# The opening of a hybrid attention and PEER layer: where the adaLN sums, the low parts and the loads are placed

## The chip, the cores and the metric

The kernel runs on one core of a Trainium2 chip. The metric is the device time of one execution in microseconds (us), the median of several runs.

## The reference, cut to what matters

One decoder layer for 256 tokens of width 1024, in float32. The part that the change touches is the opening:

```python
mod = silu(c) @ w_ada + b_ada                # (6144): sh1, sc1, g1, sh2, sc2, g2
h = rms_norm(x, norm_attn) * (1 + sc1) + sh1
proj = h @ w_in                              # MoBA q|k|v, DSA q|k|v, indexer q|k|weights
y = concat(moba_attention(...), dsa_attention(...)) @ w_out    # 16 heads of 64
x = x + g1 * y
h = rms_norm(x, norm_ffn) * (1 + sc2) + sh2
x = x + g2 * peer_ffn(h, ...)                # scores, top 16 of 256 per head, 16384 experts
out = rms_norm(x, norm_final)
```

With 256 tokens MoBA is plain causal attention; DSA keeps for each token the 64 keys that the indexer scores highest.

## The kernel before

Tokens stand along the free dimension: x is `xT`, eight tiles (c = 0 to 7) of 128 features by 256 tokens. Products that need float32 precision are done as three matmuls of rounded operands (`mm3`, lines 127 to 130): each operand is split into a high part, a rounded copy made by ScalarE (line 109), and a low part, the remainder, made by VectorE or GpSimd (line 111). `lo_engine` (line 100) names the engine of the low part of weight tile k: GpSimd for k below 9 and for 12 to 16, VectorE for the rest up to the PEER weights.

All weights come through one stream, `seq`, of 128 x 1024 tiles (512 KB), in four buffers `raw`; `load_next` issues the next one, `ahead` and `take` issue loads and splits some tiles ahead of their use. All these loads and those of `w_ada` are issued by SyncE, in order. A load that waits for its buffer holds all behind it. The first tiles of `seq` are two pairs of q and k (k = 0 to 3, the "early" tiles), four tiles of V's left half (4 to 7), and then, in the order of `ORDER`, the indexer's three and the pairs of the later heads.

`silu(c) @ w_ada` is a sum over eight chunks (128 rows of w_ada by 1024 columns, one of six parts). `ada_step` (lines 216 to 220) adds one chunk, scaled per partition by `sc`, to an accumulator on VectorE; a column of ones on TensorE then sums over the partitions (`ada_end`, line 327, which leaves mod in columns), and line 330 adds the bias. For the scale part (part 1) chunks 0 and 2 go to TensorE as rows instead (`ada_rows`, line 314) and are turned into columns at line 321.

The opening is written in a fixed order per engine (`tc.manual_schedule()`). It computes the squares' sum and the root `rstd`; the scale part, full chunks; then, half by half (four of the eight c), `xa_half`: VectorE makes xa = x * amul * rstd (line 365), ScalarE its high part xh (line 366), VectorE or for two of the c GpSimd its low part xl (line 363). `early_mm` multiplies the four early tiles with xa, before the shift is known; the shift's share is added later through `early_shift` (line 347, the shift as two columns) and `early_cols` (line 354), as a bias per output row. The shift part (part 0) is summed in column halves of 512, all eight chunks on VectorE; after each half `sh_half` makes the shifted h as hi (line 256) and lo (line 257). V's first tiles are multiplied between these (`vproj_steps`). The early products of tile 3 stand behind the first half's column sum in TensorE's order; V's second tile stands behind the second's.

`early_cols` ends the room of the early tiles; the attention's `bias` tile takes that room, and its two loads (1 MB each, from a small table `frd` in DRAM, which holds the bias by distance) follow there.

Behind the opening the framework's planner orders the instructions of each engine from the program's order and a model of their times. The program's order is `ORDER`: A computes q and k of a pair of heads, S the softmax, B the values, I, N and T the indexer's projections, norm and top-k (64 of 256 by eight rounds of max and replace), V the right half of V, D2, D3 and D4 the VectorE sums of the other modulation parts (part 2 is g1, 3 and 4 belong to the second norm), E their transposes and reduces (`ada_half`, lines 235 to 238). Then come the output projection, the second norm, PEER's scores and routing, and two long loops over 128 tiles of U and of V (lines 912, 913 and 128 to 130).

Of the kernel before, what the change touches and what calls it, by code (L numbers as in the profile page):

```python
# [16 lines left out]
T = 256  # L17
# [27 lines left out]
def hybrid_kernel(ctx, tc, io, out):  # L45
# [14 lines left out]
    def bank_a():  # L60
        return bank("pa", 2)
# [44 lines left out]

# [49 lines left out]

    def first_load(part, half, c):
        a, n = (0, 1024) if part else (half * 512, 512)
        w = first_w[part, half, c] = w0.tile([128, n], FT, tag=f"wada{part}", name="wada", bufs=6 if part else 10)
        col = part * 1024 + a  # L160
        nc.sync.dma_start(w, io["w_ada"][c * 128:(c + 1) * 128, col:col + n])

    for c in range(8):
        first_load(1, 0, c)
        if c in W_AT[0]:
            load_next()
    for half in range(2):
        for c in range(8):
            if c in W_AT[1 + half]:
                load_next()  # L170
            first_load(0, half, c)
# [126 lines left out]
    def ada_dve(part, half, chunks, w=None):  # L298

        for c in chunks:  # L300
            x = first_w[part, half, c]
            o = acc1 if part else acc0[:, half * 512:half * 512 + 512]
            if w is not None:
                x, o = x[:, w], o[:, w]
            ada_step(o, x, c, c == next(i for i in range(8) if i not in ADA_PE[part, half]))

    def ada_rows(part, half, cols):

        p = bank("c3" if half else "c2")
        chunks = ADA_PE[part, half]  # L310
        row = pf.tile([1, 512], FT, tag="row", name="row", bufs=2)
        for c in chunks:
            w = first_w[part, 0 if part else half, c]
            nc.tensor.matmul(p[0:1, :], sc[:, c:c + 1], w[:, half * 512:half * 512 + 512] if part else w,
                             start=(c == chunks[0]), stop=(c == chunks[-1]))
            yield None
        nc.scalar.activation(row, p[0:1, :], AF.Copy)
        yield None
        for q in range(4):
            w = slice(q * 128, q * 128 + 128)  # L320
            nc.tensor.matmul(cols[:, q:q + 1], row[:, w], ones[0:1, 0:1], start=(q == 0), stop=False, skip_group_check=True)
        yield None

    def ada_end(part, half, cols):

        for q in range(4):
            nc.tensor.matmul(cols[:, q:q + 1], (acc1 if part else acc0)[:, (half * 4 + q) * 128:(half * 4 + q + 1) * 128],
                             ones[:, 0:1], start=(q == 0 and not ADA_PE[part, half]), stop=(q == 3), skip_group_check=True)
        s = slice(part * 8 + half * 4, part * 8 + half * 4 + 4)
        nc.vector.tensor_tensor(mod[:, s], cols[:, 0:4], bada[:, s], op=OP.add)  # L330

# [24 lines left out]

    def xa_half(half):
        s = slice(half * 4, half * 4 + 4)
        m = slice(8 + half * 4, 12 + half * 4)
        nc.vector.scalar_tensor_tensor(amul[:, 0, s], mod[:, m], 1.0, nat[:, s], op0=OP.add, op1=OP.mult)  # L360

        def low(c):
            (nc.vector if XL_DVE[c] else nc.gpsimd).tensor_tensor(xl[:, c, :], xa[:, c, :], xh[:, c, :].bitcast(FT), op=OP.subtract)
        for c in range(half * 4, half * 4 + 4):
            nc.vector.scalar_tensor_tensor(xa[:, c, :], xT[:, c, :], amul[:, 0, c:c + 1], rstd, op0=OP.mult, op1=OP.mult)
            nc.scalar.activation(xh[:, c, :], xa[:, c, :], AF.Copy)
            if c % 4:
                low(c - 1)
        low(c)
# [20 lines left out]
    next(r10); next(r11)  # L390
    busy(BUSY1)
    next(r10); next(r11)
    busy(BUSY1)
    fps = bank_a()
    nc.tensor.matmul(fps[:16, :256], rbT, oh, start=True, stop=True)
    ada_dve(1, 0, (3,))
    rstd = next(rs)
    ada_dve(1, 0, (4, 5, 6))
    next(r10); next(r11)
# [12 lines left out]
    ada_end(1, 1, pc[1][:, 4:8])
    xa_half(1)
    early_ps = [bank_b(), bank_b(), bank("c0"), bank("c1")]
    early_mm(0, 0)
    early_mm(1, 0)
    early_mm(0, 1)
    early_mm(1, 1)
    early_split()
    early_mm(2, 0)  # L420
    early_mm(2, 1)
    early_split()
    ada_dve(0, 0, range(8))
    cols0 = bank("c2")
    ada_end(0, 0, cols0)
    ada_dve(0, 1, range(0, 2))
    early_mm(3, 0)
    early_mm(3, 1)
    sh_half(0)
    ahead(6, 2)  # L430
    shp = bank("c3")
    early_shift(0)
    ada_dve(0, 1, range(2, 8))
    cols1 = bank("c2")
# [630 lines left out]
```

## Time and profile before

| | us |
|---|---|
| median of 3 runs | 1030.16 (1029.49 to 1030.53) |
| the profiled execution | 1031.32 |
| its span, first to last instruction | 1029.50 |

```profile
PE 988.0 (96%) x5695; PEld 842.5 (82%) x5695; DVE 786.4 (76%) x1588; ACT 634.5 (62%) x1411; POOL 58.4 (6%) x78
PE   8888999989899999999999999999999999999996
DVE  5948987689999988888888898767555555555556
POOL 2442210000300000000000000000000000000000
PEclk8789989999999999999999999999999999999998
```

The first line has the busy time of each engine: PE is TensorE's matmuls, PEld its weight loads, DVE is VectorE, ACT is ScalarE, POOL is GpSimd; SP in other rows is SyncE, which issues the loads. The others divide the span into 40 slices of 25.7 us; a digit is the busy share in tenths, and for PEclk the clock that TensorE was granted, in tenths of full speed. The opening fills the first three slices.

### The profile page before, as it was taken

What the parts mean: (1) busy time and instruction counts of PE and PEld (TensorE: products, weight loads), DVE (VectorE), ACT (ScalarE), POOL (GpSimd) and SP (SyncE); (2) the same over time, 40 slices, a digit from 0 to 9 for tenths busy, and PEclk for the clock granted to TensorE, in tenths of its full rate; (3) what the DMA queues carried; (4) which work ended last, traced back from release to release, by engine and by line L of the source; (5) the groups of instructions that cost most, each with busy time, mean ns of one, the idle gap of its engine ahead of it and who ended that gap; (6) DMA issues with size and microseconds to landing.
All of it is one profiled execution on the core that took longest, in us unless ns stands there. A gap on an engine that the chain in (4) does not pass through costs nothing.

```text
span 1029.5 us, 16253 instructions
## 1 busy us (share of the span) xinstructions
PE 988.0 (96%) x5695; PEld 842.5 (82%) x5695; DVE 786.4 (76%) x1588; ACT 634.5 (62%) x1411; POOL 58.4 (6%) x78
## 2 busy tenths in 40 slices
PE   8888999989899999999999999999999999999996
PEld 6767887889778788888888888886888888888885
DVE  5948987689999988888888898767555555555556
ACT  3345566454465689988899887644545455454543
POOL 2442210000300000000000000000000000000000
PEclk8789989999999999999999999999999999999998
DMA  8557675544355565555555555578665656566561
GB/s 340 195 172 270 235 245 182 185 144 165 123 167 181 164 184 165 167 165 171 165 170 168 164 167 178 179 270 275 223 198 189 198 190 197 191 194 193 193 195 64
DMA packets 56150, 195.16 MB, mean 190 GB/s; under 512 B 6226, under 2 KB 8322, under 8 KB 55683
## 3 DMA queue, kind: packets, MB, share of 16 engines
q1 hardware_dynamic: 55778, 192.80, 57.5%
q10 hardware_dynamic: 288, 1.31, 0.3%
q8 instruction: 45, 0.74, 0.3%
q14 instruction: 39, 0.31, 0.1%
HBM read 191.97 MB, written 2.12 MB: 189 GB/s over the span
## 4 chain that ended last, share of the span: by engine, by line
PE 59%; DVE 8%; ACT 3%; DMA 2%; issue 1%; DVEq 0%; ACTq 0%
PE c L912 11%; PE c L129 10%; PE c L128 10%; PE c L130 10%; PE pa L912 7%; PE c L913 5%; PE pa L913 4%; DVE lo L111 2%; PE pb L869 1%; PE pb L870 1%; ACT hi L109 1%; DMA raw<-w_ada 1%; DMA raw<-V 1%; ACT ol L862 1%; DVE gt L919 1%
## 5 line engine op out<-in xcount | busy, mean ns | idle before, releaser
L111 DVE TENSOR_TENSOR lo<-raw,hi 128x1024 fp32r<-128x1024 f32 x290 | 354.8, 1224 | 168.5 <-ACT hi L109 167.7
L109 ACT ACTIVATE hi<-raw 128x1024 fp32r<-128x1024 f32 x303 | 320.8, 1059 | 219.4 <-PE c L130 150.9
L912 PE MATMUL c<-h,hi 128*128 128x512 f32 x608 | 219.4, 400 | 1.4 <-ACT hi L109 1.4
L129 PE MATMUL c<-lo,w 128*128 128x512 f32 x509 | 198.3, 390 | 1.6 <-DVE lo L111 1.5
L128 PE MATMUL c<-hi,w 128*128 128x512 f32 x509 | 198.6, 390 | 0.0
L130 PE MATMUL c<-hi,w 128*128 128x512 f32 x509 | 197.9, 389 | 0.0
L913 PE MATMUL c<-h,lo 128*128 128x256 f32 x608 | 159.0, 282 | 3.9 <-DVE lo L111 3.9
L912 PE MATMUL pa<-h,hi 128*128 128x512 f32 x416 | 151.7, 399 | 1.0 <-ACT hi L109 1.0
L912 PEld LDWEIGHTS c<-h,hi 128*128 128x128 f32 x608 | 113.5, 189 | 23.1 <-ACT hi L109 2.2
L913 PEld LDWEIGHTS c<-h,lo 128*128 128x128 f32 x608 | 114.9, 190 | 11.0 <-DVE lo L111 5.6
L129 PEld LDWEIGHTS c<-lo,w 128*128 128x128 f32 x509 | 95.6, 188 | 22.7 <-DVE lo L111 3.2
L128 PEld LDWEIGHTS c<-hi,w 128*128 128x128 f32 x509 | 95.5, 188 | 20.8 <-ACT hi L109 0.9
L130 PEld LDWEIGHTS c<-hi,w 128*128 128x128 f32 x509 | 95.6, 188 | 19.9
L913 PE MATMUL pa<-h,lo 128*128 128x256 f32 x416 | 108.6, 281 | 1.0 <-DVE lo L111 1.0
L912 PEld LDWEIGHTS pa<-h,hi 128*128 128x128 f32 x416 | 78.1, 188 | 15.3 <-ACT hi L109 1.5
L862 ACT ACTIVATE ol<-og,glT 128x128 f16<-128x128 f16 x256 | 88.6, 438 | 0.1
L913 PEld LDWEIGHTS pa<-h,lo 128*128 128x128 f32 x416 | 78.1, 189 | 5.9 <-DVE lo L111 2.2
L128 PE MATMUL pa<-h,hi 128*128 128x256 f32 x240 | 71.6, 298 | 3.6 <-ACT h L256 3.1
L129 PE MATMUL pa<-h,hi 128*128 128x256 f32 x240 | 70.2, 292 | 0.0
L130 PE MATMUL pa<-h,lo 128*128 128x256 f32 x240 | 69.6, 292 | 0.0
L220 DVE SCALAR_TENSOR_TENSOR acc<-wada,sc,acc 128x1024 f32<-128x1024 f32 (+1 forms) x41 | 60.3, 1473 | 4.7 <-DMA wada<-w_ada 4.1
L128 PEld LDWEIGHTS pa<-h,hi 128*128 128x128 f32 x240 | 47.5, 198 | 5.0 <-ACT h L256 3.4
(280 smaller groups left out, 1435.2 us busy)
## 6 DMA issues: line engine op xcount, KB each, us to landing
raw<-U SPq DMA_DIRECT2D x128, 512.0 KB, 3.5
raw<-V SPq DMA_DIRECT2D x128, 512.0 KB, 4.2
wada<-w_ada SPq DMA_DIRECT2D x32, 512.0 KB, 6.5
raw<-wqk SPq DMA_DIRECT2D x19, 512.0 KB, 5.5
raw<-wq SPq DMA_DIRECT2D x16, 512.0 KB, 3.6
wada<-w_ada SPq DMA_DIRECT2D x16, 256.0 KB, 6.0
raw<-wv SPq DMA_DIRECT2D x8, 512.0 KB, 5.7
raw<-wo SPq DMA_DIRECT2D x8, 512.0 KB, 4.4
```

What stands on the lines that cost most here:

```text
L109: nc.scalar.activation(hi, raw, AF.Copy)
L111: lo_eng.tensor_tensor(lo, raw, hi.bitcast(FT), op=OP.subtract)
L128: nc.tensor.matmul(ps, lh, rh, start=first, stop=False)
L129: nc.tensor.matmul(ps, lh, rl, start=False, stop=False)
L130: nc.tensor.matmul(ps, ll, rh, start=False, stop=last)
L220: nc.vector.scalar_tensor_tensor(acc, w, sc[:, c:c + 1], acc, op0=OP.mult, op1=OP.add)
L862: nc.scalar.activation(ol[:, q // 2, :, q % 2], og[:, q // 2, :, q % 2], AF.Copy, scale=glT[:, t0 + q:t0 + q + 1])
L869: nc.tensor.matmul(w[:, qs], o1[:, a, :, b], og[:, a, :, b], start=True, stop=False)
L870: nc.tensor.matmul(w[:, qs], o1[:, a, :, b], ol[:, a, :, b], start=False, stop=True)
L912: both = [lambda: nc.tensor.matmul(ps, hi[:, w], hcat[:, c].rearrange("p a t -> p (a t)"), start=(c == 0), stop=(c == 7)), lambda: nc.tens ...
L913: lambda: nc.tensor.matmul(ps[:, T:], lo[:, w], hh[:, c, :], start=False, stop=False)]
L919: nc.vector.tensor_tensor(gt, gt, ps[:, :T], op=OP.add)
```

## The change

- Loads: raw 0 and 1 come ahead of the scale part's chunks, raw 2 and 3 ahead of the shift part's. All 16 chunks are full width, in 11 buffers.
- Low parts: `lo_engine` gives VectorE every tile that GpSimd had, up to the PEER weights (the first three tiles of U stay on GpSimd); the early tiles' and xl's go to VectorE too. GpSimd keeps the additions of bias and mask in the attention.
- Scale part: chunk 4 joins 0 and 2 on TensorE. VectorE makes lo 0 and lo 1 first, then x * rstd into xa (`xr_all`), then the remaining sums. Both halves' column sums come first; then `xh_all`: ScalarE makes xh = xa * amul and VectorE xl = xa * amul - xh, c by c. ScalarE scales xa itself later (`xa_half`).
- Early products: tiles 0 and 1, then lo 2 and lo 3, then tiles 2 and 3, all ahead of the shift part's sums.
- Shift part: all eight chunks over columns 0 to 511 and the column sum, then the rest. V's first two tiles stand ahead of the second column sum.
- frd is written early. E2 stands behind B2 in `ORDER` instead of behind T. Chunks 0, 1, 5 and 6 of every later part use buffers in `pa` (for part 2 too, which had three buffers in `pf` alone and now has five in all).
- The unneeded matmuls of `busy`: 13, 2 and 2, 4 where there were 13, 3 and 3, 6.

```diff
-ORDER = "D2 S0 S1 I N B0 A2 T E2 A3 B1 S2 D4 A4 S3 B2 A5 S4 B3 A6 S5 E4 D3 A7 V B4 S6 B5 S7 B6 E3 B7"
+ORDER = "D2 S0 S1 I N B0 A2 T A3 B1 S2 D4 A4 S3 B2 E2 A5 S4 B3 A6 S5 E4 D3 A7 V B4 S6 B5 S7 B6 E3 B7"
...
-        return nc.gpsimd if k < 9 or k in LO_POOL else nc.vector
+        return nc.vector
...
-        p, n = (pf, 3) if part == 2 or c % 5 < 3 else (pa, 2)
+        p, n = (pa, 2) if c % 5 < 2 else (pf, 3)
...
+    load_next()
+    load_next()
+    for part in (1, 0):
+        for c in range(8):
+            w = first_w[part, c] = w0.tile([128, 1024], FT, tag="wada", name="wada", bufs=11)
+            nc.sync.dma_start(w, io["w_ada"][c * 128:(c + 1) * 128, part * 1024:(part + 1) * 1024])
+        if part:
+            load_next()
+            load_next()
...
+    def xr_all():
+        for c in range(8):
+            nc.vector.tensor_tensor(xa[:, c, :], xT[:, c, :], rstd, op=OP.mult)
+
+    def xh_all():
+        nc.vector.scalar_tensor_tensor(amul[:, 0, :], mod[:, 8:16], 1.0, nat, op0=OP.add, op1=OP.mult)
+        for c in range(8):
+            g = amul[:, 0, c:c + 1]
+            nc.scalar.activation(xh[:, c, :], xa[:, c, :], AF.Copy, scale=g)
+            nc.vector.scalar_tensor_tensor(xl[:, c, :], xa[:, c, :], g, xh[:, c, :].bitcast(FT), op0=OP.mult, op1=OP.subtract)
+
     def xa_half(half):
...
         for c in range(half * 4, half * 4 + 4):
+            nc.scalar.activation(xa[:, c, :], xa[:, c, :], AF.Copy, scale=amul[:, 0, c:c + 1])
...
     for c in range(8):
         square_sum(ms, xT, c)
+    early_split()
+    early_split()
     rs = rows_rsqrt_steps(ms, D)
     next(rs)
+    ada_dve(1, (1,), first=True)
+    rstd = next(rs)
+    xr_all()
+    ada_dve(1, (3, 5, 6, 7))
...
+    nc.sync.dma_start(frd, fr)
...
+    ada_end(1, 0, box[1, 0])
+    ada_end(1, 1, box[1, 1])
+    xh_all()
...
+    for half in range(2):
+        early_mm(0, half)
+        early_mm(1, half)
     early_split()
     early_split()
     xa_half(0)
     xa_half(1)
+    for k in (2, 3):
+        early_mm(k, 0)
+        early_mm(k, 1)
+    ada_dve(0, range(8), slice(0, 512), first=True)
+    ada_end(0, 0, bank("c2"))
     sh_half(0)
     ahead(6, 2)
+    ada_dve(0, range(8), slice(512, 1024), first=True)
     vg = vproj_steps(0)
     next(vg)
+    shp = bank("c2")
+    early_shift(0)
+    next(vg)
+    ada_end(0, 1, bank("c3"))
     sh_half(1)
     early_shift(1)
     early_cols()
```

## Rows read from the trace of the kernel before

**Rows 1.** Stretches: us; busy PE, PEld, DVE, ACT, POOL (x); clock, DMA share, GB/s.

```profile
0.00:73.20 73.20, 61.12 (x292) 49.75 (x292) 47.28 (x65) 26.43 (x49) 28.65 (x53) 0.81 0.65 228
73.20:119.00 45.80, 39.96 (x288) 35.66 (x288) 40.17 (x98) 25.12 (x59) 12.03 (x5) 0.96 0.79 281
```

**Rows 2.** Timeline of VectorE (DVE) in the opening: start us, us, instruction.

```profile
10.89 0.75 DVE L218 TENSOR_SCALAR acc<-wada,sc 128x1024 f32<-128x1024 f32 x1 [7.18 <-DMA wada<-w_ada]
...
13.46 1.28 DVE L220 SCALAR_TENSOR_TENSOR acc<-wada,sc,acc 128x1024 f32<-128x1024 f32 x1 [1.48 <-DMA wada<-w_ada]
...
33.04 9.88 DVE L220 SCALAR_TENSOR_TENSOR acc<-wada,sc,acc 128x512 f32<-128x512 f32 x7
...
45.08 0.75 DVE L220 SCALAR_TENSOR_TENSOR acc<-wada,sc,acc 128x512 f32<-128x512 f32 x1
...
45.81 1.67 DVE L257 SCALAR_TENSOR_TENSOR h<-xa,mod,h 128x256 fp32r<-128x256 f32 x4
47.40 10.69 DVE L220 SCALAR_TENSOR_TENSOR acc<-wada,sc,acc 128x512 f32<-128x512 f32 x6
```

**Rows 3.** Timeline of TensorE (PE) up to the first scores.

```profile
27.34 0.56 PE L128 MATMUL pb<-xh,ehi 128*128 128x256 f32 x1
...
42.97 1.48 PE L327 MATMUL c<-ones,acc 128*128 128x1 f32 x8 [3.61 <-DVE acc L220]
...
58.24 1.84 PE L327 MATMUL c<-ones,acc 128*128 128x1 f32 x8 [3.60 <-DVE acc L220]
...
73.20 0.92 PE L508 MATMUL pb<-kT,qT 64*128 64x256 f32 x8
```

**Rows 4.** Timeline of GpSimd (POOL) in the opening.

```profile
47.52 8.45 POOL L111 TENSOR_TENSOR lo<-raw,hi 128x1024 fp32r<-128x1024 f32 x3 [8.30 <-ACT hi L109]
```

**Rows 5.** Timeline of VectorE, 48.2 to 50.9: one step alone.

```profile
48.18 2.75 DVE L220 SCALAR_TENSOR_TENSOR acc<-wada,sc,acc 128x512 f32<-128x512 f32 x1
```

**Rows 6.** A stretch of the first loads.

```profile
10.00:15.00 5.00, 5.00 (x19) 1.96 (x18) 2.63 (x4) 1.04 (x3) 0.00 (x0) 1.00 1.03 415
```

**Rows 7.** Timeline of TensorE: neighbouring early matmuls at either clock.

```profile
28.97 0.41 PE L129 MATMUL pb<-xl,ehi 128*128 128x256 f32 x1
29.19 0.41 PE L130 MATMUL pb<-xh,elo 128*128 128x256 f32 x1
...
34.05 0.28 PE L129 MATMUL pb<-xl,ehi 128*128 128x256 f32 x1
34.17 0.28 PE L130 MATMUL pb<-xh,elo 128*128 128x256 f32 x1
```

**Rows 8.** Timeline of VectorE and of ScalarE: a low part, three high parts.

```profile
46.40 3.09 ACT L109 ACTIVATE hi<-raw 128x1024 fp32r<-128x1024 f32 x3
...
71.73 1.23 DVE L111 TENSOR_TENSOR lo<-raw,hi 128x1024 fp32r<-128x1024 f32 x1 [2.95 <-ACT hi L109]
```

**Rows 9.** TensorE's waits from 60 to 186 us: in total, times, longest.

```profile
PE pb L586 <- ACT rel L589: 3.4, 2, 2.9
```

**Rows 10.** Stretches at the lower clock.

```profile
19.60:33.10 13.50, 10.98 (x51) 10.60 (x51) 12.96 (x23) 4.74 (x10) 5.42 (x4) 0.50 0.73 273
104.90:108.20 3.30, 3.30 (x16) 3.30 (x17) 2.52 (x2) 0.64 (x2) 2.34 (x1) 0.50 0.98 351
135.60:142.40 6.80, 6.80 (x26) 5.44 (x25) 4.90 (x13) 2.27 (x7) 2.25 (x4) 0.50 0.90 299
```

**Rows 11.** Timeline of VectorE: the first softmax step.

```profile
74.83 0.43 DVE L518 SCALAR_TENSOR_TENSOR s<-pb,bias 128x256 f32<-128x256 f32 x1 [1.87 <-DMA bias<-frd]
```

**Rows 12.** Timeline of VectorE from 85 to 105 us.

```profile
88.74 2.97 DVE L220 SCALAR_TENSOR_TENSOR acc<-wada,sc,acc 128x1024 f32<-128x1024 f32 x1 [2.63 <-DMA wada<-w_ada]
...
100.42 2.82 DVE L592 SCALAR_TENSOR_TENSOR wk<-rel,iw,wk 128x256 f32<-128x256 f32 x2
...
103.88 0.75 DVE L592 SCALAR_TENSOR_TENSOR wk<-rel,iw,wk 128x256 f32<-128x256 f32 x2
```

**Rows 13.** Line L238: count, duration ns min/median/max, first and last start.

```profile
L238 DVE TENSOR_TENSOR mod<-mod,small x6: 142/153/2246, 98.3 to 181.6; 128x4 f32<-128x4 f32 x6
```

More of the change, by code (lines that the diff above doesn't have):

```diff
@@ L155, in hybrid_kernel @@
     first_w = {}
[L157 to L165, printed above, removed]
-            load_next()
[L167 to L171, printed above, removed]
+    load_next()
[5 more added lines that the diff above has]
+        if part:
+            load_next()
+            load_next()
     ones = cst.tile([128, 128], FT, name="ones")
@@ L296, in vproj_steps, with ada_dve, ada_rows @@
             nc.scalar.activation(v[:, tt, g * 512:(g + 1) * 512], pv[tt], AF.Copy)
-    def ada_dve(part, half, chunks, w=None):
+    def ada_dve(part, chunks, cols=slice(0, 1024), first=False):
+        o = acc1 if part else acc0
         for c in chunks:
[L301 to L307, printed above, removed]
+            ada_step(o[:, cols], first_w[part, c][:, cols], c, first and c == chunks[0])
+    def ada_rows(part, half, box):
         p = bank("c3" if half else "c2")
@@ L312, in ada_rows @@
         for c in chunks:
-            w = first_w[part, 0 if part else half, c]
-            nc.tensor.matmul(p[0:1, :], sc[:, c:c + 1], w[:, half * 512:half * 512 + 512] if part else w,
+            nc.tensor.matmul(p[0:1, :], sc[:, c:c + 1], first_w[part, c][:, half * 512:half * 512 + 512],
                              start=(c == chunks[0]), stop=(c == chunks[-1]))
@@ L318, in ada_rows @@
         yield None
+        cols = box[part, half]()
+        box[part, half] = cols
         for q in range(4):
             w = slice(q * 128, q * 128 + 128)
-            nc.tensor.matmul(cols[:, q:q + 1], row[:, w], ones[0:1, 0:1], start=(q == 0), stop=False, skip_group_check=True)
+            nc.tensor.matmul(cols[:, q:q + 1], row[:, w], ones[0:1, 0:1], start=(q == 0),
+                             stop=(q == 3 and len(chunks) == 8), skip_group_check=True)
         yield None
     def ada_end(part, half, cols):
-        for q in range(4):
-            nc.tensor.matmul(cols[:, q:q + 1], (acc1 if part else acc0)[:, (half * 4 + q) * 128:(half * 4 + q + 1) * 128],
-                             ones[:, 0:1], start=(q == 0 and not ADA_PE[part, half]), stop=(q == 3), skip_group_check=True)
+        if len(ADA_PE[part, half]) < 8:
+            for q in range(4):
+                nc.tensor.matmul(cols[:, q:q + 1], (acc1 if part else acc0)[:, (half * 4 + q) * 128:(half * 4 + q + 1) * 128],
+                                 ones[:, 0:1], start=(q == 0 and not ADA_PE[part, half]), stop=(q == 3), skip_group_check=True)
         s = slice(part * 8 + half * 4, part * 8 + half * 4 + 4)
@@ L355, in early_cols @@
         nc.vector.tensor_copy(cols, shp[:, :EARLY])
-    def xa_half(half):
[L358 to L363, printed above, removed]
-        for c in range(half * 4, half * 4 + 4):
[L365 to L369, printed above, removed]
+    def xr_all():
[7 more added lines that the diff above has]
+            nc.vector.scalar_tensor_tensor(xl[:, c, :], xa[:, c, :], g, xh[:, c, :].bitcast(FT), op0=OP.mult, op1=OP.subtract)
+    def xa_half(half):
+        for c in range(half * 4, half * 4 + 4):
+            nc.scalar.activation(xa[:, c, :], xa[:, c, :], AF.Copy, scale=amul[:, 0, c:c + 1])
     def sh_half(half):
@@ L386, in hybrid_kernel @@
         square_sum(ms, xT, c)
+    early_split()
+    early_split()
     rs = rows_rsqrt_steps(ms, D)
-    ada_dve(1, 0, (1,))
     next(rs)
[L390 to L393, printed above, removed]
+    ada_dve(1, (1,), first=True)
+    rstd = next(rs)
+    xr_all()
+    ada_dve(1, (3, 5, 6, 7))
+    for _ in range(3):
+        next(r10)
+        next(r11)
     fps = bank_a()
     nc.tensor.matmul(fps[:16, :256], rbT, oh, start=True, stop=True)
[L396 to L399, printed above, removed]
     fr = pf.tile([16, 384], FT, name="fr")
@@ L402, in hybrid_kernel @@
     nc.scalar.activation(fr[:, :256], fps[:16, :256], AF.Copy)
+    dp = pool("dp", space=bass.MemoryType.DRAM)
+    frd = dp.tile([16, 384], FT, name="frd")
+    nc.sync.dma_start(frd, fr)
+    busy(BUSY1)
     run(r10)
+    busy(BUSY1)
     run(r11)
-    ada_dve(1, 0, (7,), slice(0, 512))
-    ada_dve(1, 0, (7,), slice(512, 1024))
     busy(BUSY2)
+    ada_end(1, 0, box[1, 0])
+    ada_end(1, 1, box[1, 1])
+    xh_all()
+    early_ps = [bank_b(), bank_b(), bank("c0"), bank("c1")]
+    for half in range(2):
+        early_mm(0, half)
+        early_mm(1, half)
     early_split()
     early_split()
-    ada_end(1, 0, pc[0][:, 0:4])
     xa_half(0)
-    ada_end(1, 1, pc[1][:, 4:8])
     xa_half(1)
[L414 to L428, printed above, removed]
+    for k in (2, 3):
[3 more added lines that the diff above has]
+    ada_end(0, 0, bank("c2"))
     sh_half(0)
     ahead(6, 2)
[L431 to L434, printed above, removed]
+    ada_dve(0, range(8), slice(512, 1024), first=True)
     vg = vproj_steps(0)
     next(vg)
-    ada_end(0, 1, cols1)
+    shp = bank("c2")
+    early_shift(0)
+    next(vg)
+    ada_end(0, 1, bank("c3"))
     sh_half(1)
-    next(vg)
     early_shift(1)
@@ L447, in hybrid_kernel @@
     pa = pool("pa", stack=at_stack)
-    dp = pool("dp", stack=at_stack, space=bass.MemoryType.DRAM)
-    frd = dp.tile([16, 384], FT, name="frd")
-    nc.sync.dma_start(frd, fr)
     bias = pa.tile([128, 16, T], FT, name="bias")
```

15 lines of the change are left out of this document (6 added, 9 removed).

## The prediction

> **What bounds the kernel now.** I read the stages first, then, inside the first one, VectorE's order of time, GpSimd's beside it and TensorE's, and last the waits. The opening (adaLN sums, the scaled x, the early projections) ends at 73.20 us, when TensorE takes up the first scores [rows 3]; TensorE's granted clock averages 0.81 there [rows 1]. The reader is to see that VectorE leads this stage: TensorE twice stands 3.6 us, up to 42.97 and 58.24, for VectorE's sum over w_ada [rows 3], and the sums run almost end to end, 33.04 to 42.92 and 47.40 to 58.09 [rows 2].
>
> Those sums take longer than their instructions. One step over 512 columns is 0.75 us (45.08), one over 1024 is 1.28 (13.46) [rows 2]. The six from 47.40 take 10.69, where 6 x 0.79 (0.75 and 0.04 between) is 4.7. GpSimd makes three lo parts from 47.52 to 55.97 [rows 4], and a sum step beside one takes 2.75 [rows 5]: 2 us lost per lo part, 6.0 in all. So a VectorE instruction stands still while GpSimd works. The Trainium skill (SBUF — State Buffer, section Who interferes with whom) says that a VectorE instruction with two inputs in SBUF and a GpSimd instruction that reads SBUF contend, and that the later one waits for the whole of the other; the trace agrees, 2.75 for 0.75.
>
> After the opening TensorE is nearly full: from 73.20 to 119.00 it is busy 39.96 of 45.80 us [rows 1], and up to 186 us its longest wait is 2.9, for the indexer's rel [rows 9].
>
> **The opening, step by step.** I lay out the new order with durations of this trace, against the old times.
>
> *Queue.* raw 0 and raw 1 now precede the scale part: 1 MB at 415 GB/s [rows 6] is 2.6 us. The first sum step began at 10.89, as its load landed [rows 2], so it moves to about 13.4. Ahead of it VectorE makes lo 0 and lo 1 (1.23 each [rows 8]) in what was idle time. The shift part's loads that need a freed buffer come while the scale part is summed, and frd's 24 KB move to where nothing waits for them: I cost both at nothing, and fewer idle matmuls (BUSY) too, as TensorE waits there anyway.
>
> *Scale part.* m 0.42 from 13.3, the first step 0.75 beside ScalarE's Ln and Exp (1.0): 14.8; three steps of the root 1.4: 16.2. New: eight products of x and rstd, 0.42 each by the four steps from 45.81 [rows 2]: 19.5. Four sums of 1.30: 24.7. Chunk 4 has gone to TensorE's rows, and nothing runs on GpSimd.
>
> *To the first matmul.* Both halves' column sums now come before any scaling, 1.84 each as at 58.24 [rows 3]: 28.4; mod, amul and one ScalarE pass 0.8: 29.2, against 27.34 [rows 3], 1.9 later. From there two passes per column (ScalarE's xh, VectorE's xl) of 0.42 keep ahead of TensorE's three matmuls per column and weight. ScalarE's eight new passes for xa (3.4) lie beside the early matmuls, which take 14 us; without these they would stand ahead of the shifted h.
>
> *Early matmuls.* All 96 now stand ahead of the shift part's first column sum; before, 24 of them stood behind it. They start 0.21 apart at the lower clock and 0.12 at the upper [rows 7]. The clock was 0.50 to 33.1 [rows 10], 5.8 us after the first matmul; with the same delay it rises at 35.0: 28 matmuls until then, 68 x 0.12 = 8.2 after: 43.2. If it rises at 33.2 again, 19 and 77 x 0.12: 42.4.
>
> *Shift part, first half.* VectorE is through with xl at 32.8; lo 2 and lo 3 take 2.5, eight steps 0.5 + 7 x 0.79 = 6.0: 41.3, before 42.92. The column sum now waits for TensorE: 43.2 to 44.5, before to 44.45 [rows 3]. ScalarE's four hi and VectorE's four lo of h follow (1.7 [rows 2]), then hi 4 on ScalarE (1.03 [rows 8]), lo 4 and lo 5 on VectorE: 49.8.
>
> *Shift part, second half.* Eight steps of together 6.0: 55.8, before 58.09. TensorE meanwhile does V's first two weight tiles (12 matmuls of 512 columns each) and the first shift rows. As it pauses from 44.5 to 48.7, I count the first tile at the lower clock (0.43 a matmul, twice [rows 7]; 0.23 at the upper): 53.9; shift rows 2.5, second tile 2.8: 59.2; column sum 1.3: 60.5, before 60.1. That is 0.4 late, but V's second tile, which stood behind this sum, is done. What is left: shift rows 1.9, their columns 1.0, 24 matmuls x 0.23 = 5.5, gaps 0.5: 69.4 against 73.20, **3.8 gained**. With the clock rising as early as before (0.8) and staying up over the pause (12 x 0.2 = 2.4) it is 7.0. I take **5.0**, nearer to the first, which lets the clock fall in the pause. The bias loads wait for the room of the early tiles, so they move by the same; the first softmax step waited for them until 74.83 [rows 11].
>
> **The attention.** Five more lo parts (of wqk) leave GpSimd in 88 to 113, and cost VectorE 5 x 1.2 = 6.0. What they took there: L238, median 0.15, ran up to 2.25 [rows 13]; a pair of wk steps, 0.75 at 103.88, ran 2.82 at 100.42, and one more pair 1.8 too long; a sum step of 1.28 ran 2.97 at 88.74 [rows 12]: 2.1 + 2.1 + 1.8 + 1.7 = 7.7. E2's two reduces and adds (1.7) go to a later place. Part 2's sum gets five buffers instead of three; it waited 2.6 for a load [rows 12]. So VectorE is 7.7 + 1.7 + 2.6 - 6.0 = 6.0 better until the top-k's end and 1.7 worse behind it, where part 4 is summed. TensorE can take of that only what it idles: the 2.9 [rows 9] and, behind it, 3.3 us at clock 0.50 [rows 10], half of it lost: 4.5. The bounds: 6.0 + 1.7 lost, if TensorE waits for every lo part; 2.9 and half of both slow stretches [rows 10], 7.9, gained. I take **3.5 gained**, less than 4.5, as some lo part will stand ahead of a wk step where it stood beside it.
>
> What follows after 186 us is the same work on the same queues, relative to its start: zero.
>
> *Sum.* The profiled execution took 1031.3 (its span 1029.5): 1031.3 - 5.0 - 3.5 = 1022.8. It was 1.2 over the median of the runs: **1021.6**.
>
> A rule that speaks against the change: the Trainium skill (Perfetto Trace Analysis, section Optimizing Scalar/DVE Operations) says that work may go from a saturated VectorE even to GpSimd, with the warning that the two share a read port. The rows at 88 to 104 bear out the warning. Where VectorE reads a single tensor, as in the top-k beside the last of the five parts, the rule would hold, and rival A is what it would do.
>
> **Rivals.**
> *A, opening only.* The lo parts stood beside work that they didn't stop (the top-k's steps) often enough that moving them costs VectorE what it gives; TensorE keeps its 2.9 gap. For: one of the five stood there. Against: [rows 12, 13]. 1031.3 - 5.0 - 1.2 = 1025.1.
> *B, more.* The gap and both slow stretches close and the opening gives its 7.0: 7.0 + 7.9 = 14.9, from 1030.1: 1015.2. For: one cause, VectorE late, stands behind the gap. Against: ScalarE's exp, and not VectorE, is named by some of the shorter waits.
> *C, no change.* The planner, which orders all behind the opening, puts the five lo parts ahead of softmax steps, and TensorE waits: 6.0 lost, 5.0 gained: 1031.1. For: VectorE runs almost without a pause from 88 to 119. Against: 7.7 of that were stalls.
> *D, slower.* The clock stays at 0.50 through the early matmuls. Place: the 96 matmuls from 29.2. Price: 68 x 0.09 = 6.1, then V's 36 matmuls x 0.2 = 7.2 and shift rows 1.6, 15 in all. It decides if the clock is still 0.50 at 43 us: 1030.1 + 15 - 8.5 = 1036.6. For: it was 0.50 for 13.5 us [rows 10], and the new order feeds TensorE later. Against: from 29.2 on a matmul is always ready.
> *E, the stall isn't GpSimd's.* Then the long steps stay and seven lo parts x 1.2 come on top: 1038.5. Against: the lengths 2.75 and 2.25 match a lo part (8.45 for three [rows 4]). Counted with D.
>
> **How the numbers follow.** Forecast (1018.5 to 1024) 0.50; A (1024 to 1028) 0.17; B (below 1018.5) 0.14; C (1028 to 1032.2) 0.12; D with E 0.07. What a measurement of this kernel can tell from no change is about 0.2%, 2.1 us; faster is below 1028.1. So faster 0.81, same 0.12, slower 0.07. The range, 1015 to 1029, reaches over B and into C, and leaves out most of C, and D.
>
> **What would show it.** Right: no sum step over 512 columns above 0.8 us; GpSimd idle in the opening; the first early matmul near 29, the first scores before 71; the first softmax step near 70; TensorE's gap at the indexer below 1 us. Wrong: sum steps still above 2 us; clock 0.50 at 43 us; the softmax not earlier although the sums are; TensorE with new gaps of some us between 90 and 130 while VectorE is full.

## The result, and the profile after

The changed kernel takes 1022.19 us (median of 4 runs, 1021.99 to 1022.34); the kernel before, run beside it, 1030.21 (1029.49 to 1030.53): a ratio of 0.9921, 95% interval 0.9907 to 0.9935. That is 8.0 us faster; the forecast was 1021.6. The experiments below show that the sum was right for a reason that is only half the forecast's: the moved low parts alone are worth some 13 us, and another edit, which the forecast counted as a gain (part 2's sum gets more buffers), takes 4 to 6 of them back.

The page of the changed kernel: the first lines, and rows of the 40 slices.

```profile
PE 979.2 (96%) x5691; PEld 832.9 (82%) x5691; DVE 779.2 (76%) x1601; ACT 634.8 (62%) x1419; POOL 20.8 (2%) x62
...
POOL 0000010002100000000000000000000000000000
PEclk9799999999999999999999999999999999999999
```

GpSimd is below a tenth of every slice up to 127 us, and VectorE's busy time has fallen by 7.2 us although it now makes GpSimd's low parts too. The profiled execution took 1022.12 us, span 1020.2. Its two stages, in the columns of [rows 1]:

```profile
0.00:68.24 68.24, 58.43 (x288) 45.10 (x289) 41.92 (x73) 29.01 (x57) 3.02 (x42) 0.87 0.74 273
68.24:111.44 43.20, 36.78 (x274) 32.53 (x274) 38.39 (x102) 24.66 (x59) 0.00 (x0) 1.00 0.77 265
```

111.44 is the end of the top-k. Before it was at 119.17: 45.97 us behind the first scores, now 43.20.

VectorE's order of time, which answers to [rows 2, 11]:

```profile
13.09 0.75 DVE L208 TENSOR_SCALAR acc<-wada,sc 128x1024 f32<-128x1024 f32 x1
...
15.46 2.77 DVE L350 TENSOR_TENSOR xa<-xT,r 128x256 f32<-128x256 f32 x8
18.15 5.24 DVE L210 SCALAR_TENSOR_TENSOR acc<-wada,sc,acc 128x1024 f32<-128x1024 f32 x4
...
35.79 5.48 DVE L210 SCALAR_TENSOR_TENSOR acc<-wada,sc,acc 128x512 f32<-128x512 f32 x7
43.67 0.16 DVE L320 TENSOR_TENSOR mod<-c,small 128x4 f32<-128x4 f32 x1 [2.40 <-PE c L317]
...
49.44 5.48 DVE L210 SCALAR_TENSOR_TENSOR acc<-wada,sc,acc 128x512 f32<-128x512 f32 x7
...
58.66 0.16 DVE L320 TENSOR_TENSOR mod<-c,small 128x4 f32<-128x4 f32 x1 [1.47 <-PE c L317]
...
70.42 0.42 DVE L504 SCALAR_TENSOR_TENSOR s<-pb,bias 128x256 f32<-128x256 f32 x1 [2.09 <-DMA bias<-frd]
...
74.86 0.75 DVE L208 TENSOR_SCALAR acc<-wada,sc 128x1024 f32<-128x1024 f32 x1
```

Seven steps of the shift part take 5.48, twice, where seven took 9.88 and six 10.69. Now VectorE waits for TensorE's column sums (2.40, 1.47), not TensorE for VectorE. The last row is the first step of part 2's sum: it will matter.

TensorE's order of time, as [rows 3]; the first row is the last of the unneeded matmuls, the last one a new wait in the attention.

```profile
22.99 2.08 PE L257 MATMUL pb<-ones 128*128 128x128 f32 x8
24.86 1.71 PE L317 MATMUL c<-ones,acc 128*128 128x1 f32 x8
...
29.27 0.58 PE L125 MATMUL pb<-xh,ehi 128*128 128x256 f32 x1 [0.99 <-ACT xh L356]
...
42.68 0.95 PE L317 MATMUL c<-ones,acc 128*128 128x1 f32 x8
...
57.68 0.95 PE L317 MATMUL c<-ones,acc 128*128 128x1 f32 x8
...
68.24 0.92 PE L494 MATMUL pb<-kT,qT 64*128 64x256 f32 x8
...
111.22 0.41 PE L127 MATMUL pa<-h,lo 128*128 128x256 f32 x1 [3.56 <-DVE lo L108]
```

Stretches at the lower clock, as [rows 10]:

```profile
22.70:32.90 10.20, 9.21 (x42) 8.87 (x42) 4.47 (x12) 4.19 (x10) 0.00 (x0) 0.50 1.03 408
46.60:53.40 6.80, 6.27 (x14) 4.17 (x15) 6.54 (x9) 2.28 (x4) 0.00 (x0) 0.50 0.61 193
111.45:114.86 3.41, 3.41 (x18) 3.41 (x18) 3.41 (x11) 0.98 (x4) 2.25 (x4) 0.50 0.56 154
```

TensorE's waits from 60 to 178 us (total, times, longest), as [rows 9]:

```profile
PE pa L127 <- DVE lo L108: 3.6, 1, 3.6
...
PE pb L572 <- ACT rel L575: 0.6, 1, 0.6
```

The wait at the indexer went from 2.9 to 0.6, and another of 3.6 has come: a low part (tile 16's) that the planner put behind the whole top-k on VectorE.

Along the way the changed kernel is ahead by 5.0 us at the first scores, 7.7 at the top-k's end, 8.6 at the second norm's amul (167.11, now 158.54), and 9.3 at the end of the profiled spans (8.0 by the medians: the profiled execution of before was 1.1 above its median, that of the changed kernel at it).

### The profile page after: what moved, and what is told of

Same layout as the page of the kernel before. It is cut to its first block, busy times and chain, and to the rows that moved or that the text cites. A ratio compares the mean times of both kernels' runs of the same rounds, so it can differ in the third digit from the quotient of the medians.

```text
span 1020.2 us, 16221 instructions
## 1 busy us (share of the span) xinstructions
PE 979.2 (96%) x5691; PEld 832.9 (82%) x5691; DVE 779.2 (76%) x1601; ACT 634.8 (62%) x1419; POOL 20.8 (2%) x62
## 4 chain that ended last, share of the span: by engine, by line
PE 62%; DVE 8%; DMA 2%; ACT 2%; issue 1%; DVEq 0%; ACTq 0%
PE c L898 11%; PE c L126 10%; PE c L125 10%; PE c L127 10%; PE pa L898 8%; PE c L899 6%; PE pa L899 4%; DVE lo L108 2%; PE pb L855 1%; PE pb L856 1%; DMA raw<-w_ada 1%; DMA raw<-V 1%; ACT hi L106 1%; DVE gt L905 1%; ACT ol L848 0%
## 5 line engine op out<-in xcount | busy, mean ns | idle before, releaser
L108 DVE TENSOR_TENSOR lo<-raw,hi 128x1024 fp32r<-128x1024 f32 x300 | 366.4, 1223 | 168.7 <-ACT hi L106 167.8
L898 PEld LDWEIGHTS c<-h,hi 128*128 128x128 f32 x608 | 112.8, 188 | 22.7 <-ACT hi L106 2.1
L904 ACT ACTIVATE gt<-c 128x256 f32<-128x256 f32 x76 | 29.1, 382 | 35.9 <-PE c L898 35.6
```

Of the source, the lines that this page charges most:

```text
L108: lo_eng.tensor_tensor(lo, raw, hi.bitcast(FT), op=OP.subtract)
L898: both = [lambda: nc.tensor.matmul(ps, hi[:, w], hcat[:, c].rearrange("p a t -> p (a t)"), start=(c == 0), stop=(c == 7)), lambda: nc.tens ...
L904: nc.scalar.activation(gt, ps[:, T:], AF.Copy)
```

## The experiments

Twelve kernels ran, each beside the kernel before on the same chip, whose median was 1028.9 to 1029.8 in the three groups of four. So they are compared by their ratio to it. Where the text gives a difference in us it is one of medians; by the ratios it is at most 1.5 us another. In the table "opening" is the order of loads, sums and early products (old as before, new as changed), "part 2's buffers" the pools that its chunks use, "E2" the place of E2 in `ORDER`. The two columns of places in time are from one profiled execution each, which for e12_sum_order was 5 us faster than the median, for the others at most 2.3 off it.

| kernel | low parts | opening | part 2's buffers | E2 | first scores | from there to the top-k's end | us | ratio (95%) |
|---|---|---|---|---|---|---|---|---|
| before | GpSimd 14, xl 2 | old | pf | old | 73.20 | 45.97 | 1030.2 | 1 |
| e12_low_opening_only | GpSimd 5 | old | pf | old | 65.55 | 39.96 | 1017.11 | 0.9881 (0.9862 to 0.9900) |
| e1_low_only | VectorE | old | pf | old | 65.61 | 39.00 | 1016.26 | 0.9871 (0.9856 to 0.9885) |
| e11_low_e2_moved | VectorE | old | pf | new | 65.43 | 40.12 | 1016.01 | 0.9869 (0.9850 to 0.9888) |
| e7_low_attention_new | VectorE | old | pa, pf | new | 66.07 | 45.65 | 1022.25 | 0.9931 (0.9910 to 0.9952) |
| changed | VectorE | new | pa, pf | new | 68.24 | 43.20 | 1022.19 | 0.9921 (0.9907 to 0.9935) |
| e10_old_buffers | VectorE | new | pf | new | 68.38 | 39.50 | 1018.53 | 0.9887 (0.9869 to 0.9905) |
| e5_attention_old | VectorE | new | pf | old | 67.18 | 41.26 | 1020.46 | 0.9920 (0.9896 to 0.9944) |
| e13_tile3_first | VectorE | old, tile 3 earlier | pf | old | 66.91 | 39.12 | 1018.82 | 0.9894 (0.9877 to 0.9911) |
| e12_sum_order | VectorE | new, two orders back | pf | old | 63.55 | 40.24 | 1017.44 | 0.9883 (0.9867 to 0.9899) |
| e2_order_only | GpSimd 14 | new | pa, pf | new | 73.29 | 46.02 | 1033.68 | 1.0041 (1.0026 to 1.0057) |
| e4_low12to16_pool | GpSimd 5 | new | pa, pf | new | 68.60 | 46.75 | 1028.54 | 0.9989 (0.9978 to 1.0000) |
| e3_low16_pool | GpSimd 1 | new | pa, pf | new | 68.26 | 44.01 | 1025.97 | 0.9962 (0.9948 to 0.9975) |

**The low parts alone, and the order alone.**

```diff
 # e1_low_only, on the kernel before
-XL_DVE = [1, 1, 1, 1, 1, 0, 1, 0]
+XL_DVE = [1, 1, 1, 1, 1, 1, 1, 1]
-        return nc.gpsimd if k < 9 or k in LO_POOL else nc.vector
+        return nc.vector
 # e2_order_only, on the changed kernel
-        return nc.vector
+        return nc.gpsimd if k < 9 or 12 <= k <= 16 else nc.vector
...
-        early_w.append(split(raws.pop(k), nc.vector, ehi[:, k, :], elo[:, k, :]))
+        early_w.append(split(raws.pop(k), lo_engine(k), ehi[:, k, :], elo[:, k, :]))
```

> The kernel before with one edit: every low part that GpSimd made (tiles 0 to 8, 12 to 16, two of xl) is made by VectorE; order, loads and sums stay. Theory S (VectorE stood still while GpSimd worked, and taking GpSimd away is the gain): the scale part loses 4.3 us of stalls and takes two low parts, 2.4; the first half loses 4.4 and takes 2.4; the second loses 6.0 and takes 3.6: the first scores 5 to 6 us earlier than 73.2, no sum step over 512 columns above 0.8 us, and with the attention 1022 to 1025. Rival O (the new order of loads and products is the gain, and a low part costs VectorE what it costs): 14 low parts x 1.2 us on a full VectorE, 1034 to 1045, first scores at 80 or later.

> The changed kernel with the low parts of tiles 0 to 8 and 12 to 16 put back on GpSimd; the new order stays (xl stays on VectorE, where it is one instruction). S: four low parts (4 to 7) now stand beside the second half's sums, 2 us each; the root and the first half lose some too: first scores 5 us later than 68.2, and the attention as before: 1028 to 1031. O: 1021 to 1024, first scores near 68.

The low parts alone give more than the whole change, which no theory had, and the order alone is slower than before, also outside what was expected. What the forecast overlooked stands in the trace of before, ahead of the first early matmul (timelines of VectorE and GpSimd):

```profile
15.92 9.63 DVE L220 SCALAR_TENSOR_TENSOR acc<-wada,sc,acc 128x1024 f32<-128x1024 f32 x5
...
18.57 2.36 POOL L111 TENSOR_TENSOR elo<-raw,ehi 128x1024 fp32r<-128x1024 f32 x1 [16.00 <-ACT ehi L109]
22.19 2.81 POOL L111 TENSOR_TENSOR elo<-raw,ehi 128x1024 fp32r<-128x1024 f32 x1 [1.26 <-ACT ehi L109]
```

VectorE with the low parts alone:

```profile
15.36 5.39 DVE L220 SCALAR_TENSOR_TENSOR acc<-wada,sc,acc 128x1024 f32<-128x1024 f32 x5
20.67 2.35 DVE L111 TENSOR_TENSOR elo<-raw,ehi 128x1024 fp32r<-128x1024 f32 x2
...
34.47 0.75 DVE L218 TENSOR_SCALAR acc<-wada,sc 128x1024 f32<-128x1024 f32 x1
...
62.24 2.74 DVE L220 SCALAR_TENSOR_TENSOR acc<-wada,sc,acc 128x1024 f32<-128x1024 f32 x2
```

The same five steps of the scale part: 9.63 beside two low parts of GpSimd, 5.39 without. The first early matmul comes at 24.31 instead of 27.34 (0.6 of it is a first load that landed earlier: the first sum step is at 10.32 for 10.89). And another sum has moved into the opening: part 2's first step is at 34.47, and six of its eight are done by 65 us. Before, the first was at 79.36. This is the planner's order and not only idle time that came free: before, SyncE issued part 2's first load at 69.64, behind the bias loads, now at 26.02. Why the planner moves these loads when the low parts change their engine is not shown.

With the low parts back on GpSimd, the new order keeps the shift part's stalls: seven steps take 9.53 in the first half, and in the second:

```profile
47.22 13.46 DVE L210 SCALAR_TENSOR_TENSOR acc<-wada,sc,acc 128x512 f32<-128x512 f32 x7
```

**Is it GpSimd's reading?** The changed kernel, with work on GpSimd whose output nobody uses: memsets beside the first half's sum, subtractions beside the second's. The two additions over four columns only make GpSimd wait for its turn.

```diff
...
+    nc.gpsimd.tensor_tensor(spare[:, :4], elo[:, 3, :4].bitcast(FT), elo[:, 3, :4].bitcast(FT), op=OP.add)
+    for _ in range(4):
+        nc.gpsimd.memset(spare, 0.0)
     ada_dve(0, range(8), slice(0, 512), first=True)
...
+    nc.gpsimd.tensor_tensor(spare[:, :4], hl[:, 3, :4].bitcast(FT), hl[:, 3, :4].bitcast(FT), op=OP.add)
+    for _ in range(4):
+        nc.gpsimd.tensor_tensor(spare.rearrange("p (c t) -> p c t", c=2), xT[:, 0:2, :], xT[:, 2:4, :], op=OP.subtract)
     ada_dve(0, range(8), slice(512, 1024), first=True)
```

> The changed kernel with idle work put on GpSimd beside the shift part's sums: four memsets of 128x512 (no input) beside the first half's steps, four subtractions of 128x512 with two inputs in SBUF beside the second half's. Theory S: VectorE's two-input steps stand still while GpSimd reads SBUF: the second half's steps, 0.75 each now, stretch to the length of a subtraction (1.5 to 3 us for up to four of them), so that the second column sum comes 3 to 7 us later than 57.7; the first half's steps stay at 0.75. Rival 1: any work of GpSimd, reading or writing, stops them: both halves stretch. Rival 2: only the low parts did (their type or size): neither half stretches.

It ran once (1029.13 us), so it is its trace that counts. Timelines of GpSimd and VectorE:

```profile
33.31 2.28 POOL L420 MEMSET spare<- 128x512 f32 x4
...
44.21 7.12 POOL L427 TENSOR_TENSOR spare<-xT 128x512 f32<-128x512 f32 x4
...
33.23 5.47 DVE L210 SCALAR_TENSOR_TENSOR acc<-wada,sc,acc 128x512 f32<-128x512 f32 x7
...
44.24 4.54 DVE L108 TENSOR_TENSOR lo<-raw,hi 128x1024 fp32r<-128x1024 f32 x2 [0.46 <-ACT hi L106]
48.70 1.49 DVE L208 TENSOR_SCALAR acc<-wada,sc 128x512 f32<-128x512 f32 x1
50.23 6.37 DVE L210 SCALAR_TENSOR_TENSOR acc<-wada,sc,acc 128x512 f32<-128x512 f32 x7
```

The memsets lie beside the first three of the seven steps, which keep their 5.47. Beside the subtractions (44.21 to 51.33) the two low parts take 4.54 for 2.36, the first step 1.49 for 0.48, the next seven 6.37 for 5.48: 4.1 us lost. A GpSimd instruction that reads stops VectorE, one that only writes does not. The subtractions began earlier than intended and hit the low parts first; and since TensorE's work covers some of it, the second column sum moved only 2.5 us (from the first half's mod to the second's: 17.5 for 15.0), below the 3 to 7 expected. The Trainium skill (SBUF — State Buffer, section Who interferes with whom) says that a GpSimd instruction that only writes SBUF leaves VectorE's two-input steps alone, and that tensor_scalar can enter a mode that contends too; the rows agree with both (5.47, and 1.49 for 0.48).

**The new wait at 111 us.** GpSimd gets tile 16's low part back, or those of tiles 12 to 16.

```diff
-        return nc.vector
+        return nc.gpsimd if k == 16 else nc.vector          # e3_low16_pool
+        return nc.gpsimd if 12 <= k <= 16 else nc.vector    # e4_low12to16_pool
```

> The changed kernel with the low part of tile 16 alone back on GpSimd. In the changed kernel the planner put it behind the whole top-k on VectorE, 10.5 us after its high part, and TensorE stood 3.6 us for it at 107.66, with 3.4 us at the lower clock behind. The top-k's steps read one tensor and should not be stopped. If that wait is on the path: gap gone, up to 3.6 + 1.7 = 5.3 us, 1017 to 1019.5. Rival: the next low part or the softmax behind the top-k holds TensorE as long: 1021.3 to 1022.8.

> The changed kernel with the attention's five low parts, tiles 12 to 16, back on GpSimd; the opening as changed. S: the first scores stay at 68.2; from there the stalls at the sum of part 2 and at the indexer's steps come back (7.7 us of VectorE for 6.0 saved), but tile 16 is free of the top-k: TensorE's gap at the indexer (2.9 us) returns and the one at 107.66 goes: 1021 to 1024. If the attention's gain of 4 us came from these five low parts alone: 1025 to 1027. If all of the attention's gain has other causes (buffers, E2) and tile 16 is the price: 1017 to 1019.5.

Both are misses: slower, by 3.8 and 6.4 us. In the first, the wait for the low part is gone, but the planner's new order waits 2.5 for a softmax step near the same place, and the time rises. So removing that one wait does not give its 3.6 us. In the second, the sum steps between first scores and top-k's end, in the changed kernel and with five low parts on GpSimd:

```profile
L210 DVE SCALAR_TENSOR_TENSOR acc<-wada,sc,acc 128x1024 f32<-128x1024 f32 x8 | 10.2, 1278 | 0.0
```

```profile
L210 DVE SCALAR_TENSOR_TENSOR acc<-wada,sc,acc 128x1024 f32<-128x1024 f32 x8 | 16.4, 2056 | 0.0
```

Eight steps lose 6.2 us, and TensorE waits 5.1 for one of them. But with the old opening and the old buffers the same five cost next to nothing:

```diff
 # e12_low_opening_only, on the kernel before, with XL_DVE all 1
-        return nc.gpsimd if k < 9 or k in LO_POOL else nc.vector
+        return nc.gpsimd if k in LO_POOL else nc.vector
```

> The kernel before with the low parts of tiles 0 to 8 and of xl on VectorE, those of tiles 12 to 16 left on GpSimd. Theory S: each low part that runs on GpSimd beside VectorE costs, in the attention as in the opening. Then the first scores keep the 65.6 of the kernel with all of them moved, the stretch from there to the top-k's end goes back from 39 to about 45 as before, and the time is 1021 to 1023.5. Rival: the five of the attention are hidden, and the attention got shorter only because the opening ended earlier: stretch 39 to 41, time 1016 to 1018.5.

Theory S falls, the rival holds: 1017.11 against 1016.26, with overlapping intervals. The stretch from the first scores to the top-k's end, here and with all low parts moved:

```profile
65.55:105.51 39.96, 37.23 (x268) 33.19 (x268) 32.94 (x96) 23.38 (x57) 12.72 (x5) 0.96 0.77 281
```

```profile
65.61:104.61 39.00, 37.29 (x278) 33.32 (x278) 33.83 (x100) 24.59 (x59) 0.00 (x0) 1.00 0.75 275
```

VectorE is busy 33 of 40 us in both: there is room for a stall. In the changed kernel it is busy 38.4 of 43.2, with ten sum steps there for four. So what a stall costs seems to depend on how much of part 2's sum is left for this stretch. This is argued: the two pairs of kernels differ in the opening, the buffers and E2 too, and no run has the five low parts on GpSimd with the new opening and the old buffers.

**Buffers or E2?** The square's other corners, and each half by itself.

```diff
 # e10_old_buffers and e5_attention_old, on the changed kernel; e7 is the reverse, on e1
-        p, n = (pa, 2) if c % 5 < 2 else (pf, 3)
+        p, n = (pf, 3) if part == 2 or c % 5 < 3 else (pa, 2)
 # e5_attention_old alone, besides; e7 and e11 the reverse, on e1
-ORDER = "D2 S0 S1 I N B0 A2 T A3 B1 S2 D4 A4 S3 B2 E2 A5 S4 B3 A6 S5 E4 D3 A7 V B4 S6 B5 S7 B6 E3 B7"
+ORDER = "D2 S0 S1 I N B0 A2 T E2 A3 B1 S2 D4 A4 S3 B2 A5 S4 B3 A6 S5 E4 D3 A7 V B4 S6 B5 S7 B6 E3 B7"
```

> The changed kernel with E2 back behind T and with the old buffers for the modulation sums; opening and low parts as changed. The low parts alone, in the old order, gave 1016.26; the changed kernel is at 1022.2, 6 slower, with its first scores 2.6 us later and 4.2 us more from the first scores to the end of the top-k. Theory S: both the rebuilt opening and the rearranged attention cost something. Then the stretch from the first scores to the top-k's end falls from 43.2 to about 39 with first scores unchanged at 68.2, and the time is 1017 to 1019.5. Rival R: the rearranged attention is harmless, and the later opening alone set the planner on a worse order: stretch 42 to 44, time 1021 to 1023.5.

> The low parts alone (old opening), with E2 behind B2 and the new buffers: the fourth corner of the square of opening (old, rebuilt) and attention (old, rearranged), all with the low parts on VectorE. Theory S (the rearrangement costs): first scores 65.6 as with the low parts alone, stretch to the top-k's end 42 to 43 in place of 39, time 1018.5 to 1021. Rival R (the rearrangement is harmless): stretch 38.5 to 39.5, time 1015 to 1017.5; the whole loss of 6 us then belongs to the opening.

> The changed kernel with one line back: part 2's chunks use the three buffers in pf again, none in pa. Theory P: the room of pa comes free only when the opening ends, so with the new buffers chunk 0 of part 2 can't be loaded, and its sum can't start, while VectorE idles in the opening (first step at 74.86 in the changed kernel, 55.59 with the low parts alone). With the line back four steps of part 2 should run before the first softmax step, the stretch from the first scores to the top-k's end falls from 43.2 to about 41, and the time is 1018.5 to 1021. Rival E: the loss is E2's new place; then the steps start early but the time stays at 1021.5 to 1023.5.

> The low parts alone (old opening, old buffers) with E2 behind B2. With E2 and the buffers both moved it took 1022.25, with neither 1016.26. Theory P (the buffers): part 2's first step stays at 55.6, stretch from the first scores to the top-k's end 37.5 to 39.5, time 1014.5 to 1017. Rival E (E2's place): stretch 43 to 46, time 1019.5 to 1022.5.

Moving E2 changes nothing that can be told (1016.01 for 1016.26). The buffers are the loss: 6.2 us with the old opening (1022.25 for 1016.01), 3.7 with the rebuilt one (1022.19 for 1018.53). Why, the first step of part 2 shows, with the new buffers in the old opening (first fence) and with the old ones in the new opening (second):

```profile
73.54 0.75 DVE L218 TENSOR_SCALAR acc<-wada,sc 128x1024 f32<-128x1024 f32 x1
```

```profile
61.88 0.75 DVE L208 TENSOR_SCALAR acc<-wada,sc 128x1024 f32<-128x1024 f32 x1
62.66 1.28 DVE L210 SCALAR_TENSOR_TENSOR acc<-wada,sc,acc 128x1024 f32<-128x1024 f32 x1
```

`pa` takes the room of the early tiles, so it exists only from the end of the opening on (in the changed kernel the bias loads, which need it too, go out at 64.32, two of part 2's chunks behind them at 65.38; the three in `pf` went out from 49.42 on). Chunk 0, the sum's first, now has its buffer there. With the old buffers six of eight steps run before the first softmax in the old opening, four in the new one; with the new buffers none, in either. They come back between the first scores and the top-k: ten sum steps of parts 2 and 4 there with the changed kernel, eleven in e7, four with the low parts alone. So e7 shows what the low parts bring without the early sum: first scores 7.1 earlier, and behind them the old stretch (45.65 for 45.97); about half of the 13 us of the low parts alone is the early sum. The edit also changes which chunks of the later parts lie in `pa`; what that is worth was not tried. (The expectations gave 55.6 for part 2's first step with the low parts alone; it is the third. The first is at 34.47.) In e10 the fall in time, to 1018.53, lies at the edge of what was expected, and its stretch fell further than it, to 39.50. That e5, with E2 in its old place, is 2 us above e10 stays open: their intervals overlap.

**What the rebuilt opening itself does.** With the old buffers it is 2.5 us behind the old one (1018.53 for 1016.01), with the new ones level (1022.19 for 1022.25). On e5_attention_old two orders were put back, one on VectorE and one on TensorE:

```diff
     ada_end(0, 0, bank("c2"))
+    ada_dve(0, range(2), slice(512, 1024), first=True)
     sh_half(0)
     ahead(6, 2)
-    ada_dve(0, range(8), slice(512, 1024), first=True)
+    ada_dve(0, range(2, 8), slice(512, 1024))
...
     early_shift(0)
-    next(vg)
     ada_end(0, 1, bank("c3"))
     sh_half(1)
+    next(vg)
```

> The rebuilt opening with the old attention (1020.46), with two steps of the shift part's second half put ahead of the first half's shifted h, where VectorE waits 2.4 us for the column sum, and the second column sum put back ahead of V's second tile on TensorE. Theory Q: these two orders are why the rebuilt opening is 4 us behind the old one with the same low parts: second column sum at 53 to 54.5 in place of 56.7, first softmax step at 68 to 69 in place of 71.3, time 1017 to 1019. Rival: the first early matmul, 4 us later than with the old opening, sets it: first scores no earlier than 66.5, time 1019.5 to 1021.5.

1017.44 for 1020.46, as theory Q has it, with intervals that touch. But the wait for the first column sum, which theory Q wanted to fill, is still there (2.54): the addition that waits for it stands ahead of the two steps. What they fill is the short waits behind it (0.27, 0.23 and 0.46 in the changed kernel). The second column sum, now ahead of V's second tile on TensorE, comes at 51.23 (57.68 in the changed kernel), earlier than theory Q's 53 to 54.5. Which of the two orders gives how much is not separated:

```profile
41.18 0.16 DVE L320 TENSOR_TENSOR mod<-c,small 128x4 f32<-128x4 f32 x1 [2.54 <-PE c L317]
41.26 0.48 DVE L208 TENSOR_SCALAR acc<-wada,sc 128x512 f32<-128x512 f32 x1
```

This trace is of the fastest of its runs (1012.59; the others 1016.9 to 1018.1): in it the clock stays up longer around the column sums, so its first early matmul is at 26.64, and of its gain at the first scores a part is that. How large a part is open.

The reverse was tried too, the changed kernel's early order on the kernel with the low parts alone:

```diff
     early_split()
+    early_mm(3, 0)
+    early_mm(3, 1)
     ada_dve(0, 0, range(8))
...
     ada_dve(0, 1, range(0, 2))
-    early_mm(3, 0)
-    early_mm(3, 1)
```

> The low parts alone with the early products of tile 3 ahead of the shift part's first column sum, as the change has them. With the low parts alone TensorE waits 4.58 us there (36.36 to 40.95) and multiplies tile 3 behind it at the lower clock in 5.2 us. Theory T: 24 matmuls at 0.12 fit into the wait; TensorE then waits for V's first low part until 46.9; first scores 63.5 to 64.6 in place of 65.6, time 1014 to 1016. Rival: the pause from 42.6 to 46.9 keeps the clock at the lower level for V's first tile too (12 x 0.2 = 2.4) and takes it back: first scores 65.5 to 67, time 1016 to 1018.5.

1018.82 (ratio 0.9894, 0.9877 to 0.9911) for 1016.26: 2.6 slower, a little beyond the rival, with intervals that overlap, and with first scores at 66.91, as the rival has it. The wait is only moved, on to the second column sum (first fence, TensorE's timeline), and the clock falls behind it (second, a stretch: TensorE's busy time, clock, DMA share, GB/s):

```profile
40.86 1.05 PE L327 MATMUL c<-ones,acc 128*128 128x1 f32 x8 [2.07 <-DVE acc L220]
...
52.99 1.02 PE L327 MATMUL c<-ones,acc 128*128 128x1 f32 x8 [3.22 <-DVE acc L220]
```

```profile
53.00:60.00 7.00, 7.00 (x28) 0.76 0.83 300
```

With the low parts alone TensorE waits 0.34 there and the clock stays at 1.00 from 48 to 67. Here an early product that is held back fills TensorE while VectorE sums.

The fastest two, e1_low_only and e11_low_e2_moved, beat the kernel before by about 13 us and the changed one by 5 to 6; e12_low_opening_only, e12_sum_order and e10_old_buffers beat both too.

## Why the prediction was right, point by point

- **GpSimd's reads stop VectorE.** Right: no 512-column step of the shift part is above 0.8 us, and the probe shows it directly. Rival E is out.
- **Queue and scale part.** Right within 1.3 us: first sum step 13.09 (13.4), root 15.4 (16.2), sums done 23.4 (24.7; the eight products take 2.77, not 3.3, and 1 MB at 415 GB/s is 2.5 us, not 2.6). First early matmul 29.27 (29.2), by a balance: the column sums began only at 24.86, as the unneeded matmuls, which the prediction put at nothing, ran on TensorE up to then, the clock at 0.50 from 22.7 on.
- **Early matmuls and pause.** Right: clock up at 32.9 (33.2 or 35.0), matmuls done at 42.7 (42.4 to 43.2). TensorE pauses from 43.6 to 46.7, and V's first tile runs at the lower clock, to 53.4 (53.9). Rival D is out.
- **Second half.** The second column sum is at 57.68 (59.2 to 60.5), the first scores at 68.24 (69.4 by the slow count, 68.2 by the value taken). The term, 5.0, measured 4.96; first softmax 70.42 (near 70).
- **But that term is two of opposite sign.** The low parts alone bring the first scores to 65.6, 7.6 earlier; the rest of the change gives 2.6 of it back. The prediction held the new order against a first matmul at 27.34 that carried 3 us of stall (24.31 without it, 0.6 of that by the earlier load; the five steps of 9.63 were not looked at), so the order seemed to cost only 1.9 there.
- **The attention: sum right, terms wrong.** Taken 3.5; measured 4.3 in the pair of profiles (the lead of 9.3 at the spans' end less the 5.0 at the first scores), 3.0 by the medians. The step that failed is "Part 2's sum gets five buffers instead of three; it waited 2.6 for a load", counted as 2.6 gained: the wait is gone, but with the low parts moved the buffers cost 3.7 to 6.2, because two of the five don't exist during the opening. E2's new place is worth nothing that can be told. The five low parts' net of 1.7 is 0.9, within the uncertainty, with the old opening and buffers, and 6.4 with the new ones.
- **VectorE's 6.0 until the top-k's end** measured 2.8 (45.97 to 43.20). The stalls, E2's steps and the wait for a load are out of that stretch, as counted, but ten sum steps stand there for eight (2.0 us), and eight low parts where VectorE and GpSimd together made seven (1.2). That the total still came near is in part luck.
- **What had no term** is that the planner can move part 2's sum. With the old buffers (e10) the stretch to the top-k's end is 39.50, 6.5 shorter than before, as half of part 2's sum is done in the opening. The prediction counted the stalls where they stood, not where the work would stand without them. The new buffers give that up, and what is left is near the 3.5: the indexer's gap closed, as forecast, and the 3.6 gap for a low part opened, which the prediction had named as a sign against itself.
- **Behind 186 us: zero.** The lead grew by 0.8 us from the second norm's amul to the end, in one pair of profiles.

## What to carry to other kernels

Hold each edit against a kernel that has the others: once the stalls are gone, a new order may be worth less than the one it replaces, and a right total can hide two wrong terms. Before a sum gets more buffers, ask from when on their room exists; the first chunk waits for it, and the whole sum with it. Idle time of an engine off the path still does work: what VectorE can't sum inside the opening it sums in the stretch where it has no room for one more stall.

## What the runs showed of the hardware that was not expected

- With the same instructions in front, the granted clock from 20 to 25 us was 0.77 in the changed kernel, 0.89 in e5_attention_old and 1.00 in e12_sum_order, and the first early matmul came at 29.27, 28.29 and 26.64. The scale part's two column sums took 1.71 and 1.84 us in the first, 0.95 and 1.03 in the last. A fall of the clock that hits the path here costs up to 2.6 us, and one profile doesn't tell whether it will.
- A step with one tensor as its input, the TENSOR_SCALAR, was held by GpSimd's reads too (1.49 for 0.48 over 512 columns, and 2.81 for 0.75 over 1024 in e2_order_only); four memsets of GpSimd, 2.28 us in all, held nothing.
